# Queuing the prompt's attention visits behind given projection chunks in a gated Conformer and dilated-attention step

## The chip, the cores and the metric

The kernel runs on one core of a Trainium2 chip. TensorE (PE) multiplies matrices, VectorE (DVE), ScalarE (ACT) and GpSimd (POOL) do the elementwise work, SyncE (SP) issues transfers; ScalarE and GpSimd issue transfers too. The metric is the device time of one execution in microseconds, as the median of repeated runs.

## What is computed

One inference step of a decoder layer, for a prompt of 1024 tokens and for 8 sequences of 8 sample tokens (64 columns), with shared weights. Projection, convolution and attention, shortened:

```python
def in_projection(x, w_in, b_in):
    h = jnp.einsum('bsd,de->bse', x, w_in) + b_in
    a_val, a_gate, z_a, q, k, v, z_b, g_a, g_b = jnp.split(h, offs, axis=-1)
    u = a_val * jax.nn.sigmoid(a_gate)
    ...
# branch A: depthwise causal convolution of u, width 31, over 1024 channels
# branch B: 3 groups (window, dilation) = (128,1), (512,4), (2048,16), 8 heads of 64 each
def dilated_prompt(q, k, v, window, dil, slopes):
    s = jnp.einsum('bnirhd,bnjrhd->bnrhij', qb, kk)
    s = jnp.where(valid, s + bias, -jnp.inf)
    lse = jax.nn.logsumexp(s, axis=-1)
    p = jnp.exp(s - lse[..., None])
    o = jnp.einsum('bnrhij,bnjrhd->bnirhd', p, vv)
    ...
def combine_groups(outs, lses):
    w = jax.nn.softmax(jnp.stack(lses, axis=2), axis=2)
    return jnp.sum(w[..., None] * jnp.stack(outs, axis=2), axis=2)
# sample tokens: the same attention over caches of keys and values plus the new tokens' own
# y = LayerNorm(ALPHA * x + W_out(sig(g_a) * W_a(conv * silu(z_a)) + sig(g_b) * W_b(attn * silu(z_b))))
```

## The kernel before

All matmuls of the projections are done in two parts of each operand (`hi` and `lo`, written by ScalarE and VectorE from a loaded weight `raw`), three matmuls for each of 8 depth tiles: 24 matmuls make a *chunk* of 384 or 352 columns of the 1088 (prompt and sample tokens together), and three chunks make one row of output features. A chunk goes to one of three accumulators `mm`, which ScalarE or VectorE empties.

A *unit* is a head pair f (0 to 3) and a group g (0 to 2); its queries and keys are two rows of three chunks (`project_qk`), its values come with those of its group (`project_v`, nine steps a group, stored to DRAM as `vd` and loaded again as `vt`). The attention of a unit goes in *bursts* of query tiles: 4, 3 and 2 bursts for g = 0, 1, 2, so 36 over all units. One *visit* of TensorE does three things in a row: the transposes `PT` of the burst before, the values `O` of the burst before that, and the scores `S` of a new one. Between visits VectorE takes bias and minimum from the scores (`P`, `st`), ScalarE takes the exponentials, and both copy the transposed tiles. When the three groups of an f are done, `combine` weighs them: the scores' minima and sums of groups 1 and 2 are stored by GpSimd (`scr`), loaded again in another layout (`stn`), and VectorE makes `mn`, `e`, `el`, `den` and `w` from them, with one exponential of ScalarE between `e` and `el`; `w` is transposed, stored (`wd`), spread (`wb`) and multiplied into the values.

A *convolution channel block* c (0 to 7) is a gate row (sigmoid on ScalarE into `ub`) and a value row (multiplied into `ub` on VectorE), then 31 taps on VectorE, each a wide one of 1024 elements and a narrow one of 64, into one accumulator slot `cv`. Two slots of `ub` are used in turn: even c has one, odd c the other. Blocks 0 to 4 are recorded after units 2, 4, 6, 8 and 11, blocks 5 to 7 in the sample phase that follows the prompt's attention, where rows of scores over the cached keys (`kv`) stand between projection chunks.

The order on each engine is made by a scheduler that simulates the program with priorities; visits have a high priority, taps a low one. The steps that this text speaks of are, by line: 189 projection matmuls, 349 scores, 378 and 386 transposes and their copies, 402 values, 359 and 366 minima and exponentials, 117 and 118 the splits `hi` and `lo`, 433 the store of the group-2 scores, 449 the load `stn`, 459 the second `mn`, 463 its exponential, 514 the gate's sigmoid, 535 and 538 taps, 552 the sample tokens' own scores, 666 the sample phase's scores.

Of the kernel before, what the change touches and what calls it, by code (L numbers as in the profile page):

```python
# [36 lines left out]
B_CONV = (2, 4, 6, 8, 11)  # L37
# [4 lines left out]
def trunk_kernel(ctx, tc, I, O):  # L42
# [211 lines left out]

    def project_v(g):
# [22 lines left out]
        for t in range(9):  # L278
            ps = mm_ps()
            st = slot(rotate("vst", (12, 13)), [P, 512], n="vst")  # L280
            if t < 8:
# [4 lines left out]
                for i, (a, b) in enumerate(ops):  # L286
                    pe.matmul(ps, a, b, start=(i == 0), stop=(i == len(ops) - 1))  # L287
                dve.tensor_tensor(out=st, in0=ps, in1=vb, op=ALU.add)  # L288
                pool.dma_start(out=vd[g, c], in_=st)
                if t * P >= n0:  # L290
                    pool.dma_start(out=O[f"vt{g}"][t * P - n0:(t + 1) * P - n0], in_=st)
            else:
                ops = [(XP[:, k].rearrange("p a n -> p (a n)"), w[k]) for k in range(KT) for w in (wh, wl)]
                for i, (a, b) in enumerate(ops):
                    pe.matmul(ps, a, b, start=(i == 0), stop=(i == len(ops) - 1))  # L295
# [5 lines left out]
                pool.dma_start(out=O[f"vt{g}"][NP_ - n0:], in_=st[:NS])  # L301

# [132 lines left out]
    def prompt_attention(f, g, q, k, vt, scr):  # L435
# [4 lines left out]
        un = {"g": g, "q": q, "k": k, "vt": vt, "scr": scr, "bias": bias, "st": st, "og": og, "tiles": qtiles(g)}  # L440
        for b in BURSTS[g]:
            visit({"unit": un, "tiles": b})
        return og, st if g == 0 else scr
# [116 lines left out]
    def project_qk(u):  # L560
# [5 lines left out]
        if first:  # L566
            for c0, cn in CHUNKS:
                for (w, ev) in zip(first, evs):
                    ev(0, c0, cn, proj_chunk([(*w, xhi, xlo)], c0, cn))
        else:  # L570
            in_proj(F_Q + i3, evs[0])
            in_proj(F_K + i3, evs[1])
# [9 lines left out]
        qk[u] = new  # L582

    w01 = [(w0, w1)]
    project_qk(0)
    project_qk(1)
    project_v(0)
    credit[1] = 1.7
    for u, (f, g) in enumerate(units):
        if g == 0:  # L590
            res = []
        q, k = qk.pop(u)
        sample_new_scores(f, g, q, k)
        scr = None if g == 0 else dram.tile([NP_, 4], F32, name=nm("scr"))
        res.append(prompt_attention(f, g, q, k, load_v(f, g), scr))
        if g == 0 and todo:
            combine(*todo.pop())
        if u + 2 < len(units):
            project_qk(u + 2)
        if u < 2:  # L600
            project_v(u + 1)
            if u == 1:
# [523 lines left out]
```

## Time and profile before

| | |
|---|---|
| median of 3 runs | 1420.6 us (1413.33 to 1421.51) |
| the profiled execution | 1418.53 us, span 1416.8 us |
| TensorE busy | 1397.8 us (99%) |
| VectorE busy | 844.1 us (60%) |
| ScalarE busy | 444.6 us (31%) |
| GpSimd busy | 159.1 us (11%) |
| mean granted clock of TensorE | 0.997 of full speed |

Busy time is the union of an engine's instructions, and the span goes from the first to the last of them; 1.7 us of the execution lie around the span. Idle time of an engine that others don't wait for costs nothing.

### The profile page before, as it was taken

The page shows a single profiled execution, that of the slowest core. Times are in us where ns is not written, and L with a number is a line of the kernel's source. Part 1 is how long each engine was busy: PE and PEld are TensorE (multiplying, and loading weights), DVE is VectorE, ACT ScalarE, POOL GpSimd, SP SyncE. Part 2 cuts the span into 40 slices and gives each one's busy share as a digit, 9 for nine tenths or more (in the row PEclk, how much of TensorE's full clock was granted, in tenths as well). Part 3 has the DMA queues.
Part 4 walks back from the last instruction along what each step waited for, and adds up shares of the span by engine and source line. Part 5 has one row for each costly group of instructions (what it writes and reads, how often), then busy time and mean ns, then how long its engine had stood idle before and what let it go on. Part 6 is the DMA issues. An engine that isn't in the chain of part 4 may idle for free.

```text
span 1416.8 us, 21922 instructions
## 1 busy us (share of the span) xinstructions
PE 1397.8 (99%) x8682; PEld 1265.6 (89%) x8682; DVE 844.1 (60%) x1632; ACT 444.6 (31%) x984; POOL 159.1 (11%) x302
## 2 busy tenths in 40 slices
PE   9999999999999999999999999999999999999997
PEld 8988888899998899999877878788899999999886
DVE  4223131329958879599989794681267526335686
ACT  5204041234433534346531213122246422103220
POOL 2010111110111110112161302000000000000000
PEclk9999999999999999999999999999999999999999
DMA  6629285266755574665489677686653436434322
GB/s 232 213 102 336 116 305 200 87 223 200 221 179 185 176 224 135 225 202 169 122 257 342 243 274 257 206 303 223 202 187 137 161 111 225 146 93 149 127 90 74
DMA packets 85110, 271.27 MB, mean 191 GB/s; under 512 B 20912, under 2 KB 40688, under 8 KB 83600
## 3 DMA queue, kind: packets, MB, share of 16 engines
q1 hardware_dynamic: 70704, 147.16, 31.8%
q10 hardware_dynamic: 2816, 87.30, 17.5%
q0 software_dynamic: 11488, 35.42, 7.6%
q8 instruction: 68, 1.11, 0.3%
q14 instruction: 34, 0.28, 0.1%
HBM read 236.39 MB, written 120.74 MB: 252 GB/s over the span
## 4 chain that ended last, share of the span: by engine, by line
PE 82%; DVE 9%; DMA 4%; issue 3%; ACT 1%; POOL 0%; SPq 0%; DVEq 0%; ACTq 0%; POOLq 0%
PE mm L189 56%; PE mm L287 9%; PE mm L967 7%; DVE cv L538 4%; PE O L666 2%; PE S L666 1%; PE S L349 1%; PE O L402 1%; PE PT L378 1%; DMA wb<-wd 1%; DVE P L359 1%; ACT P L366 1%; DMA stn<-scr 1%; DVE lo L118 1%; PE mm L295 1%
## 5 line engine op out<-in xcount | busy, mean ns | idle before, releaser
L189 PE MATMUL mm<-x,hi 128*128 128x352 f32 (+1 forms) x3648 | 909.7, 330 | 0.9 <-ACT x L117 0.4
L189 PEld LDWEIGHTS mm<-x,hi 128*128 128x128 f32 x3648 | 641.5, 188 | 43.1 <-issue 23.7
L189 PE MATMUL mm<-x,lo 128*128 128x352 f32 (+1 forms) x1824 | 598.2, 328 | 0.0
L189 PEld LDWEIGHTS mm<-x,lo 128*128 128x128 f32 x1824 | 342.2, 188 | 6.1 <-issue 4.7
L538 DVE SCALAR_TENSOR_TENSOR cv<-ub,conv_w,cv 128x1024 f32<-128x1024 f32 x240 | 306.6, 1278 | 2.0
L117 ACT ACTIVATE hi<-raw 128x1024 fp32r<-128x1024 f32 (+2 forms) x88 | 86.1, 980 | 279.4 <-PE mm L189 239.3
L118 DVE TENSOR_TENSOR lo<-raw,hi 128x1024 fp32r<-128x1024 f32 (+2 forms) x88 | 98.9, 1124 | 112.0 <-ACT hi L117 110.5
L287 PE MATMUL mm<-vhi,x 128*128 128x512 f32 x384 | 119.1, 390 | 0.0
L366 ACT ACTIVATE P<-P,st 128x128 f32<-128x128 f32 (+1 forms) x192 | 84.2, 440 | 73.0 <-DVE st L359 61.7
L287 PEld LDWEIGHTS mm<-vhi,x 128*128 128x128 f32 x384 | 72.1, 188 | 15.1 <-issue 0.2
L288 DVE TENSOR_TENSOR vst<-mm,vb 128x512 f32<-128x512 f32 x24 | 16.6, 692 | 102.9 <-PE mm L287 102.9
L287 PE MATMUL mm<-vlo,x 128*128 128x512 f32 x192 | 74.9, 390 | 0.0
L540 DVE SCALAR_TENSOR_TENSOR cv<-keep,conv_w,cv 128x64 f32<-128x64 f32 x240 | 67.8, 282 | 3.2
L787 ACT ACTIVATE gst<-mm,b_in 128x352 f32<-128x352 f32 (+1 forms) x48 | 26.7, 559 | 114.8 <-PE mm L189 83.3
L359 DVE CUSTOM_DVE_ANT_0 P<-S,bias 128x128 f32<-128x128 f32 (+1 forms) x192 | 55.0, 346 | 10.4 <-PE S L349 10.4
L967 PE MATMUL mm<-wol,mh 128*128 128x512 f32 (+1 forms) x152 | 57.4, 378 | 0.0
L967 PE MATMUL mm<-woh,mh 128*128 128x512 f32 (+1 forms) x152 | 57.4, 378 | 0.0
L967 PE MATMUL mm<-woh,ml 128*128 128x512 f32 (+1 forms) x136 | 51.2, 377 | 0.0
L684 POOL COPY qf<-keep 64x16 f32<-64x16 f32 x96 | 45.9, 490 | 38.7 <-PE S L666 35.4
L287 PEld LDWEIGHTS mm<-vlo,x 128*128 128x128 f32 x192 | 36.0, 188 | 7.5 <-issue 0.2
L378 PE MATMUL PT<-ident,P 128*128 128x128 f32 x280 | 36.9, 274 | 5.5 <-ACT P L366 5.4
L386 DVE COPY PT<-PT 128x512 f32<-128x512 f32 x36 | 24.6, 684 | 28.4 <-PE PT L378 26.1
(185 smaller groups left out, 1309.7 us busy)
## 6 DMA issues: line engine op xcount, KB each, us to landing
out_nb_dram<-in_cache_dram ACTq DMA_DIRECT2D x64, 1020.0 KB
raw<-in_w_in_dram SPq DMA_DIRECT2D x66, 512.0 KB
kv<-in_g3k_dram SPq DMA_DIRECT2D x32, 512.0 KB
kv<-in_g3v_dram SPq DMA_DIRECT2D x32, 512.0 KB
out_nb_dram<-in_cache_dram ACTq DMA_DIRECT2D x16, 1008.0 KB
kv<-in_g2k_dram SPq DMA_DIRECT2D x16, 512.0 KB
kv<-in_g2v_dram SPq DMA_DIRECT2D x16, 512.0 KB
raw<-in_w_v_dram SPq DMA_DIRECT2D x12, 512.0 KB
```

What stands on the lines that cost most here:

```text
L117: h = act.activation(out=dst_hi, in_=src, func=AF.Copy)
L118: dve.tensor_tensor(out=dst_lo, in0=src, in1=dst_hi.bitcast(F32), op=ALU.subtract)
L189: done[0] = pe.matmul(ps[:, :cn], a, b, start=(i == 0), stop=(i == len(ops) - 1))
L287: pe.matmul(ps, a, b, start=(i == 0), stop=(i == len(ops) - 1))
L359: dve.tensor_tensor_reduce(out=pr[:, h, c], in0=ps[:, h, c], in1=un["bias"][:, h, b0:b0 + nk], scale=-1.0, scalar=3e38, op0=ALU.add, op1=A ...
L366: x["exp"] = act.activation(out=pr[:, h, c], in_=pr[:, h, c], func=AF.Exp, scale=-1.0, bias=st[:, t, h, 0:1], accum_out=st[:, t, h, 1:2])
L378: m = pe.transpose(pp[:, i * P:(i + 1) * P], x["pr"][:, h, c:c + P], ident)
L538: dve.scalar_tensor_tensor(out=acc[:, :NP_], in0=ub[:, j:j + NP_], scalar=w, in1=acc[:, :NP_], op0=ALU.mult, op1=ALU.add)
L540: dve.scalar_tensor_tensor(out=accs, in0=us[:, :, j:j + 8], scalar=w, in1=accs, op0=ALU.mult, op1=ALU.add)
L666: m = pe.matmul(ps[rr], w(rr), t(r), start=start, stop=stop, tile_position=(0, rr.start), **kw)
L684: pool.tensor_copy(out=qfull(g)[hs, f].rearrange("p (r j h) -> p r j h", r=4, j=4)[:, :, :, 2 * f + h2], in_=qs[hs, g * 4 + f, 16 * pr:16 ...
L967: pe.matmul(ps[:, :cn], a, b, start=(j == 0), stop=(j == len(ops) - 1))
```

## The change

The visits are no longer placed by the scheduler's priorities. A generator (`beside`) hands out the projections and convolutions in steps, most of them one chunk: values of group g (9 steps) and queries and keys of unit 2+g (6 steps) for g = 0 to 2, then queries and keys of units 5 to 11 with the convolution blocks 0 to 4 among them (`PAIRS`), 6 steps each. Before each burst so many steps are taken that their sum is the number in `VISITS` (from the tenth burst on, 2.75 more for each), and the visit is queued behind the last matmul of the last step. The sample tokens' own scores stand in the first visit of their unit, in an accumulator of the projections and with one store pattern. A unit's values are loaded at its second burst. The combine of f is recorded after the second burst of the next f's first unit. After the last burst two more steps stand before each of the two visits that finish it.

```diff
-B_CONV = (2, 4, 6, 8, 11)
+PAIRS = ((5,), (6, 7), (8, 9), (10, 11), ())
+VISITS = (3, 6, 12, 16, 20, 24, 29, 34, 39)
 W_CONV = ((5,), (6,), (7,), ())
...
     def project_v(g):
...
-                    pe.matmul(ps, a, b, start=(i == 0), stop=(i == len(ops) - 1))
+                    done[0] = pe.matmul(ps, a, b, start=(i == 0), stop=(i == len(ops) - 1))
                 dve.tensor_tensor(out=st, in0=ps, in1=vb, op=ALU.add)
                 pool.dma_start(out=vd[g, c], in_=st)
...
+                yield
...
-    def prompt_attention(f, g, q, k, vt, scr):
+    def prompt_unit(f, g, q, k, scr):
...
-        for b in BURSTS[g]:
-            visit({"unit": un, "tiles": b})
-        return og, st if g == 0 else scr
+        return un, (og, st if g == 0 else scr)
...
     def sample_new_scores(f, g, q, k):
-        t = half("sb", [NS, 2, NS], 2)
-        ps = s_ps()
+        t = half("sb", [P, NS], 2)
+        ps = mm_ps()[:, :NS]
         for h in range(2):
             hs = slice(64 * h, 64 * h + 64)
-            pe.matmul(ps[:NS, h, :NS], q[hs, NP_:], k[hs, NP_:], start=True, stop=True)
-        act.activation(out=t, in_=ps[:NS, :, :NS], func=AF.Copy)
-        pool.dma_start(out=snew[g, 2 * f:2 * f + 2].rearrange("h q k -> q h k"), in_=t)
+            pe.matmul(ps[hs], q[hs, NP_:], k[hs, NP_:], start=True, stop=True)
+        act.activation(out=t, in_=ps, func=AF.Copy)
+        pool.dma_start(out=snew[g, 2 * f:2 * f + 2].rearrange("h q k -> (h q) k"), in_=t)
...
-    project_qk(0)
-    project_qk(1)
-    project_v(0)
-    credit[1] = 1.7
+    def beside():
+
+        for g in range(3):
+            yield from project_v(g)
+            if g == 0:
+                credit[1] = 1.7
+            yield from project_qk(2 + g)
...
+        for c in range(5):
+            for x in PAIRS[c]:
+                yield from project_qk(x)
+            yield from conv_channels(c)
+
+    for u in range(2):
+        for _ in project_qk(u):
+            pass
+    fill = beside()
+    steps = 0
+    n = 0
     for u, (f, g) in enumerate(units):
         if g == 0:
             res = []
-        q, k = qk.pop(u)
-        sample_new_scores(f, g, q, k)
-        scr = None if g == 0 else dram.tile([NP_, 4], F32, name=nm("scr"))
-        res.append(prompt_attention(f, g, q, k, load_v(f, g), scr))
-        if g == 0 and todo:
-            combine(*todo.pop())
-        if u + 2 < len(units):
-            project_qk(u + 2)
...
-        if u in B_CONV:
-            c = B_CONV.index(u)
-            for _ in conv_channels(c):
-                pass
+        for bi, burst in enumerate(BURSTS[g]):
+            n += 1
+
+            while steps < (VISITS[n - 1] if n <= len(VISITS) else VISITS[-1] + 2.75 * (n - len(VISITS))) or (u not in qk):
+                next(fill, None)
+                steps += 1
+            if bi == 0:
+                q, k = qk[u]
+                scr = None if g == 0 else dram.tile([NP_, 4], F32, name=nm("scr"))
+                un, r = prompt_unit(f, g, q, k, scr)
+                res.append(r)
+            elif bi == 1:
+                while ("v", g) not in ready:
+                    next(fill, None)
+                    steps += 1
+                un["vt"] = load_v(f, g)
+            with tc.issue_after(done[0].ins):
+                visit({"unit": un, "tiles": burst})
+                if bi == 0:
+                    sample_new_scores(f, g, q, k)
+            if todo and g == 0 and bi == 1:
+                combine(*todo.pop())
         if g == 2:
             attn[f] = slot(14 + f, [P, NT], n="attn")
             todo.append((f, res))
-    visit()
-    visit()
+    for _ in range(2):
+        for _ in range(2):
+            next(fill, None)
+        with tc.issue_after(done[0].ins):
+            visit()
+    for _ in fill:
+        pass
```

ScalarE at the end of the prompt's attention, with and ahead of the sigmoids of convolution block 5's gate (`mm_712`, `mm_715` and `mm_718` are its three chunks). `P` are exponentials, `PT` and `og` copies, `hi` weight splits, `e_738` and `PT_743` belong to the last combine, `sb` is the copy of the sample tokens' own scores. Before:

```order
L117 ACTIVATE hi_710_6218<-raw_709_6216 128x1024
L384 ACTIVATE PT_651_5725<-PT_653_5732 128x512
L366 ACTIVATE P_656_5753,st_638_5639<-P_656_5753,st_638_5639 128x256 x4
L514 ACT_TABLE_LOAD
L514 ACTIVATE ub_705_6207<-mm_712_6222,b_in_34_198 128x384
L553 ACTIVATE sb_657_5762<-S_658_5763 64x128
L384 ACTIVATE PT_664_5776<-PT_666_5783 128x512
L514 ACTIVATE ub_705_6207<-mm_715_6256,b_in_34_198 128x352
L366 ACT_TABLE_LOAD
```

After:

```order
L120 ACTIVATE hi_710_6218<-raw_709_6216 128x1024
L469 ACTIVATE e_738_6563<-e_738_6563 128x48
L428 ACTIVATE og_660_5766<-O_694_6139 128x8x64
L120 ACTIVATE hi_752_6607<-raw_751_6605 128x1024
L480 ACTIVATE PT_743_6584<-PT_742_6582 48x128
L520 ACT_TABLE_LOAD
L520 ACTIVATE ub_705_6207<-mm_712_6222,b_in_34_198 128x384
L520 ACTIVATE ub_705_6207<-mm_715_6256,b_in_34_198 128x352
L520 ACTIVATE ub_705_6207<-mm_718_6290,b_in_34_198 128x288
```

The sigmoids stood between the last unit's exponentials, and the last combine's exponential came well behind them; now they stand behind the last combine's exponential and the copy of its transposed weights.

VectorE at the same place, around the last combine's `mn_737`. `cv_688` before is block 4's accumulator (it reads `ub_675`, block 4); `cv_656` after is block 3's (it reads `ub_637`). `ub_669` after and `ub_705` before are emptied value chunks of blocks 4 and 5. Before:

```order
L519 SCALAR_TENSOR_TENSOR ub_705_6207<-mm_726_6395,b_in_34_198,ub_705_6207 128x288
L519 SCALAR_TENSOR_TENSOR keep_236_2032<-mm_726_6395,b_in_34_198,keep_236_2032 128x8x8
L538 SCALAR_TENSOR_TENSOR cv_688_6051<-ub_675_5873,conv_w_38_206,cv_688_6051 128x1024
L118 TENSOR_TENSOR lo_766_6712<-raw_764_6709,hi_765_6711 128x1024
L540 SCALAR_TENSOR_TENSOR cv_688_6051<-keep_236_2032,conv_w_38_206,cv_688_6051 128x64
L459 TENSOR_TENSOR mn_737_6562<-mn_737_6562,stn_736_6558 128x16
L538 SCALAR_TENSOR_TENSOR cv_688_6051<-ub_675_5873,conv_w_38_206,cv_688_6051 128x1024
L540 SCALAR_TENSOR_TENSOR cv_688_6051<-keep_236_2032,conv_w_38_206,cv_688_6051 128x64
L461 TENSOR_TENSOR e_738_6563<-mn_737_6562,stn_736_6558 128x16 x3
L538 SCALAR_TENSOR_TENSOR cv_688_6051<-ub_675_5873,conv_w_38_206,cv_688_6051 128x1024
```

After:

```order
L430 COPY og_660_5766<-O_691_6036 128x8x64
L465 TENSOR_TENSOR mn_737_6562<-mn_737_6562,stn_736_6558 128x16
L544 SCALAR_TENSOR_TENSOR cv_656_5698<-ub_637_5482,conv_w_38_206,cv_656_5698 128x1024
L467 TENSOR_TENSOR e_738_6563<-mn_737_6562,stn_736_6558 128x16 x3
L544 SCALAR_TENSOR_TENSOR cv_656_5698<-ub_637_5482,conv_w_38_206,cv_656_5698 128x1024
L525 SCALAR_TENSOR_TENSOR ub_669_5821<-mm_692_6046,b_in_34_198,ub_669_5821 128x288
L525 SCALAR_TENSOR_TENSOR keep_299_2452<-mm_692_6046,b_in_34_198,keep_299_2452 128x8x8
L121 TENSOR_TENSOR lo_711_6219<-raw_709_6216,hi_710_6218 128x1024
L471 TENSOR_TENSOR el_739_6564<-e_738_6563,stn_736_6558 128x16 x3
L544 SCALAR_TENSOR_TENSOR cv_656_5698<-ub_637_5482,conv_w_38_206,cv_656_5698 128x1024
```

The last combine stood among the taps of block 4, behind the last value chunk of block 5; now it stands among the taps of block 3, and the last value chunk of block 4 comes behind it.

ScalarE around the exponential of the first combine (`e_315` before, `e_289` after). `mm_262` is the third chunk of a unit's queries. Before:

```order
L213 ACTIVATE qkv_256_2145<-mm_267_2266,b_in_34_198 128x4x88
L117 ACTIVATE hi_274_2335<-raw_273_2333 128x1024
L154 DMA out_nb2_dram<-in_cache2_dram 16x16320 x2
L213 ACTIVATE qkv_256_2145<-mm_268_2292,b_in_34_198 128x4x72
L213 ACTIVATE qkv_256_2145<-mm_268_2292,b_in_34_198 128x64
L463 ACTIVATE e_315_2727<-e_315_2727 128x48
L514 ACT_TABLE_LOAD
L514 ACTIVATE ub_269_2322<-mm_276_2341,b_in_34_198 128x384
```

After:

```order
L374 ACTIVATE P_253_2126,st_228_1895<-P_253_2126,st_228_1895 128x128 x8
L216 ACTIVATE qkv_255_2144<-mm_260_2154,bq8_216 128x4x96
L216 ACTIVATE qkv_255_2144<-mm_261_2180,bq8_216 128x4x88
L469 ACTIVATE e_289_2413<-e_289_2413 128x48
L120 ACTIVATE hi_303_2457<-raw_302_2455 128x1024
L157 DMA out_nb2_dram<-in_cache2_dram 16x16320 x2
L392 ACTIVATE PT_266_2237<-PT_268_2244 128x512
L216 ACTIVATE qkv_255_2144<-mm_262_2206,bq8_216 128x4x72
L216 ACTIVATE qkv_255_2144<-mm_262_2206,bq8_216 128x64
L559 ACTIVATE sb_272_2274<-mm_273_2275 128x64
```

The exponential stood behind both rows of that unit (`qkv_255`, `qkv_256`) and ahead of a gate; now it stands between the second and the third chunk of the first row, and the copy of the third chunk (`mm_262`) comes behind it.

## Rows read from the trace of the kernel before

**Rows 1.** The page of the profile: its span, part 1 (busy time of each engine, its share of the span, instructions) and the first line of part 4 (the chain that ended last, shares of the span by engine).

```profile
span 1416.8 us, 21922 instructions
...
PE 1397.8 (99%) x8682; PEld 1265.6 (89%) x8682; DVE 844.1 (60%) x1632; ACT 444.6 (31%) x984; POOL 159.1 (11%) x302
...
PE 82%; DVE 9%; DMA 4%; issue 3%; ACT 1%; POOL 0%; SPq 0%; DVEq 0%; ACTq 0%; POOLq 0%
```

**Rows 2.** The waits of TensorE over the whole span: who waited, for what; us in total, times, longest us.

```profile
PE PT L378 <- ACT P L366: 5.4, 3, 3.0
PE S L666 <- DMA kv<-in_g3k_dram: 2.0, 2, 1.0
```

**Rows 3.** TensorE in order of time from 458 to 466 us. Columns: start us, length us, engine, line, operation, output<-inputs, tiles, count, and in brackets the idle time before it and what ended it.

```profile
458.13 0.32 PE L189 MATMUL mm<-x,hi 128*128 128x352 f32 x1
461.43 0.88 PE L378 MATMUL PT<-ident,P 128*128 128x128 f32 x6 [2.97 <-ACT P L366]
462.23 1.83 PE L402 MATMUL O<-PT,vt 128*64 128x128 f32 x16
464.00 2.02 PE L349 MATMUL S<-qkv,qkv 64*128 64x256 f32 x8
```

**Rows 4.** TensorE in order of time, same columns: one visit in mid-kernel, and further on one row of the sample phase's scores.

```profile
656.15 1.03 PE L378 MATMUL PT<-ident,P 128*128 128x128 f32 x8
657.11 1.09 PE L402 MATMUL O<-PT,vt 128*64 128x128 f32 x16
658.13 1.13 PE L349 MATMUL S<-qkv,qkv 64*128 64x256 f32 x8
659.20 0.43 PE L189 MATMUL mm<-x,lo 128*128 128x352 f32 x1
...
700.97 1.06 PE L666 MATMUL S<-kv,qf 128*32 128x512 f32 x8 [0.98 <-DMA kv<-in_g3k_dram]
```

**Rows 5.** Busy time by engine in two stretches (all engines). Columns: stretch, its length, busy us and instructions of PE, PEld, DVE, ACT and POOL, then the granted clock as a share of full speed, DMA share, GB/s.

```profile
462.40:465.80 3.40, 3.40 (x24) 2.45 (x22) 3.37 (x7) 1.45 (x2) 0.00 (x0) 0.50 0.07 22
997.70:1021.80 24.10, 24.10 (x146) 23.71 (x144) 5.76 (x5) 3.78 (x6) 0.53 (x1) 1.00 0.59 196
```

**Rows 6.** The instructions of line 552 (the sample tokens' own scores), and the idle time of their engine before them: us, times.

```profile
L552 PE MATMUL S<-qkv,qkv x48: 218/242/268, 102.6 to 676.8; 64*64 64x64 f32 x48
...
  issue: 2.6, 10
```

**Rows 7.** GpSimd in order of time: the stores of the group-2 scores (`scr`), one per combine, and one load behind them (`stn`). Columns as in rows 3.

```profile
287.68 1.36 POOL L433 DMA_DIRECT2D scr<-st  x2 [16.95 <-ACT P L366]
...
437.29 1.35 POOL L433 DMA_DIRECT2D scr<-st  x2 [6.01 <-ACT P L366]
...
568.47 1.35 POOL L433 DMA_DIRECT2D scr<-st  x2 [11.80 <-ACT P L366]
...
701.14 1.34 POOL L433 DMA_DIRECT2D scr<-st  x2 [18.79 <-ACT P L366]
...
708.93 0.92 POOL L449 DMA_DIRECT2D stn<-scr  x1 [4.45 <-issue]
```

**Rows 8.** VectorE in order of time: the four `mn` steps that wait for the loaded scores.

```profile
305.99 0.17 DVE L459 TENSOR_TENSOR mn<-mn,stn 128x16 f32<-128x16 f32 x1 [12.14 <-DMA stn<-scr]
...
451.21 0.17 DVE L459 TENSOR_TENSOR mn<-mn,stn 128x16 f32<-128x16 f32 x1 [6.64 <-DMA stn<-scr]
...
580.54 0.18 DVE L459 TENSOR_TENSOR mn<-mn,stn 128x16 f32<-128x16 f32 x1 [0.55 <-DMA stn<-scr]
...
717.00 0.17 DVE L459 TENSOR_TENSOR mn<-mn,stn 128x16 f32<-128x16 f32 x1 [3.86 <-DMA stn<-scr]
```

**Rows 9.** VectorE in order of time behind the second of them, same columns.

```profile
451.30 1.28 DVE L538 SCALAR_TENSOR_TENSOR cv<-ub,conv_w,cv 128x1024 f32<-128x1024 f32 x1
452.50 0.34 DVE L461 TENSOR_TENSOR e<-mn,stn 128x16 f32<-128x16 f32 x3
452.75 1.28 DVE L538 SCALAR_TENSOR_TENSOR cv<-ub,conv_w,cv 128x1024 f32<-128x1024 f32 x1
453.95 1.22 DVE L118 TENSOR_TENSOR lo<-raw,hi 128x1024 fp32r<-128x1024 f32 x1
...
459.05 0.17 DVE L467 TENSOR_TENSOR den<-den,el 128x16 f32<-128x16 f32 x1
459.14 0.28 DVE L359 CUSTOM_DVE_ANT_0 P<-S,bias 128x128 f32<-128x128 f32 x1
```

**Rows 10.** How long the transfers take from issue to landing (min, median, max, us): first those of line 433 (`scr`), then those that write `stn`.

```profile
DMA to landing us min/median/max: 5.8/6.8/8.4
...
DMA to landing us min/median/max: 2.7/3.5/8.6
```

**Rows 11.** The last scores of the last unit on TensorE, then the table load and the first of eight exponentials of them on ScalarE (start us, length us, and so on).

```profile
692.08 1.16 PE L349 MATMUL S<-qkv,qkv 64*128 64x128 f32 x16
...
696.36 1.28 ACT L366 ACT_TABLE_LOAD   x1 [1.93 <-DVE st L359]
697.65 0.40 ACT L366 ACTIVATE P<-P,st 128x128 f32<-128x128 f32 x1
```

**Rows 12.** The first tap of convolution block 4 on VectorE, then the first sigmoid of convolution block 5 on ScalarE.

```profile
670.82 0.81 DVE L535 TENSOR_SCALAR cv<-ub,conv_w,conv_b 128x1024 f32<-128x1024 f32 x1 [0.98 <-DMA cvd<-cv]
...
677.94 0.58 ACT L514 ACTIVATE ub<-mm,b_in 128x384 f32<-128x384 f32 x1
```

More of the change, by code (lines that the diff above doesn't have):

```diff
@@ L253, in trunk_kernel @@
     XP = None
+    ready = set()
     def project_v(g):
@@ L294, in project_v @@
                 for i, (a, b) in enumerate(ops):
-                    pe.matmul(ps, a, b, start=(i == 0), stop=(i == len(ops) - 1))
+                    done[0] = pe.matmul(ps, a, b, start=(i == 0), stop=(i == len(ops) - 1))
                 act.activation(out=st[:NS], in_=ps[NS:], func=AF.Copy)
@@ L301, in project_v @@
                 pool.dma_start(out=O[f"vt{g}"][NP_ - n0:], in_=st[:NS])
+                ready.add(("v", g))
+                yield
     def load_v(f, g):
@@ L439, in prompt_attention @@
         og = slot(rotate("O", (8, 9, 10, 11)), [P, NP_], n="og")
-        un = {"g": g, "q": q, "k": k, "vt": vt, "scr": scr, "bias": bias, "st": st, "og": og, "tiles": qtiles(g)}
-        for b in BURSTS[g]:
-            visit({"unit": un, "tiles": b})
-        return og, st if g == 0 else scr
+        un = {"g": g, "q": q, "k": k, "scr": scr, "bias": bias, "st": st, "og": og, "tiles": qtiles(g)}
+        return un, (og, st if g == 0 else scr)
     def combine(f, res):
@@ L569, in project_qk @@
                     ev(0, c0, cn, proj_chunk([(*w, xhi, xlo)], c0, cn))
+                    yield
         else:
-            in_proj(F_Q + i3, evs[0])
-            in_proj(F_K + i3, evs[1])
+            for x, ev in zip((F_Q, F_K), evs):
+                w = load_w(I["w_in"][x + i3], D)
+                for ci, (c0, cn) in enumerate(CHUNKS):
+                    ev(ci, c0, cn, proj_chunk([(*w, xhi, xlo)], c0, cn))
+                    if x == F_Q or ci < 2:
+                        yield
         pool.tensor_copy(out=qs[:, i3, :], in_=new[0][:, NP_:])
@@ L582, in project_qk @@
         qk[u] = new
+        yield
     w01 = [(w0, w1)]
-    project_qk(0)
-    project_qk(1)
-    project_v(0)
-    credit[1] = 1.7
+    def beside():
[4 more added lines that the diff above has]
+            yield from project_qk(2 + g)
+        keep[1] = slot(19, [P, NT], n="keep")
+        usv.extend(keep[i][:, c:c + 304].rearrange("p (b t) -> p b t", b=8) for i, c in ((0, 12 * NS), (1, 0), (1, 304)))
+        for c in range(5):
[8 more added lines that the diff above has]
+    n = 0
     for u, (f, g) in enumerate(units):
@@ L591, in trunk_kernel @@
             res = []
-        q, k = qk.pop(u)
-        sample_new_scores(f, g, q, k)
-        scr = None if g == 0 else dram.tile([NP_, 4], F32, name=nm("scr"))
-        res.append(prompt_attention(f, g, q, k, load_v(f, g), scr))
-        if g == 0 and todo:
-            combine(*todo.pop())
-        if u + 2 < len(units):
-            project_qk(u + 2)
-        if u < 2:
-            project_v(u + 1)
-            if u == 1:
-                keep[1] = slot(19, [P, NT], n="keep")
-                usv += [keep[i][:, c:c + 304].rearrange("p (b t) -> p b t", b=8)
-                        for i, c in ((0, 12 * NS), (1, 0), (1, 304))]
-        if u in B_CONV:
-            c = B_CONV.index(u)
-            for _ in conv_channels(c):
-                pass
+        for bi, burst in enumerate(BURSTS[g]):
[19 more added lines that the diff above has]
+                combine(*todo.pop())
         if g == 2:
```

## The prediction

> **What bounds the kernel now.** I read the page first: TensorE is busy 99% of the span and TensorE work is 82% of the chain that ended last [rows 1], so time is lost or won only where TensorE stands still or runs slowly. Second, the waits of TensorE [rows 2]: over the whole span it waited 5.4 us for exponentials (`P`), 2.0 us for the sample phase's keys (`kv`) and little else. Third, the largest of these waits in order of time [rows 3]: transposes that could have started near 458.4 start at 461.43, and the values and scores behind them take 1.83 and 2.02 us, where the same steps elsewhere take 1.09 and 1.13 [rows 4]. The granted clock says why: 0.50, the lower of the two levels (1.2 GHz), from 462.4 to 465.8, after some 3 us without work [rows 5]. Fourth, what TensorE was waiting for: VectorE stood 6.64 us at `mn L459`, the second step of a combine, until the groups' scores were back from DRAM, and the next visit's scores were queued behind it [rows 8, 9].
>
> So the kernel is a dense stream of projection chunks with visits strewn in; there is little to win, and the question is where the new order puts long waits of VectorE and ScalarE in front of something that TensorE needs.
>
> **What the change removes.** (1) Visits are now 2 to 4 chunks apart. A chunk is 24 matmuls; 146 matmuls of all widths take 24.10 us [rows 5], so 4.0 us for a chunk and 8 to 12 us between visits, in which scores, exponentials and the copy of the transposed tiles fit. The three waits on `P` (5.4 us) and the stretch at half clock should go. The latter cost 1.83+2.02 against 1.09+1.13, that is 1.6 us. (2) The sample tokens' own scores no longer stand alone between projection matmuls: TensorE lost 2.6 us in ten issue gaps ahead of their groups [rows 6]. In a visit these gaps have no reason to exist; I take 2.5. (3) The two waits on `kv`, 2.0 us, belong to visits that stood in the sample phase; I take them as gone here and price what stands there now separately. Sum: 5.4+1.6+2.5+2.0 = 11.5 us. With nothing lost elsewhere that gives 1418.5-11.5 = 1407.0.
>
> **What it moves, and where that waits.** The combine of each f used to be recorded after the whole first unit of the next f; now it comes after that unit's second burst, so its VectorE and ScalarE steps stand closer to the scores that they need. The delay from the issue of the group-2 scores' store on GpSimd to `mn` is in all four combines long: 287.68 to 305.99, 437.29 to 451.21, 568.47 to 580.54, 701.14 to 717.00 [rows 7, 8], which is 18.3, 13.9, 12.1 and 15.9 us, mean 15.0. It is a store, a load behind it on the same queue, and the time that each takes to land [rows 10].
>
> *The handoff to the sample phase (f=3).* Let τ be when TensorE reaches the transposes of the last unit's first burst. From the new order, with 4.0 to 4.1 us for a chunk and 3.05 for a visit [rows 4, 5]: last scores done at τ+18.4 (two visits, three chunks). In the trace 7.9 us went from the end of these scores to the store, 693.24 to 701.14, with a table load and eight exponentials and 1.9 us of waiting for VectorE [rows 7, 11]; with part of that wait I take 6.7: store at τ+25.1, `mn` at τ+40.1 with the mean delay. Behind `mn` VectorE still has 15 wide taps of convolution block 3: six among the steps up to the weights `w`, nine after. By [rows 9] a tap is 1.2 us, a `lo` 1.2 and the small steps 0.1 to 0.3, so the weights are done 10.3 us and the last tap 22.4 us after `mn`: τ+62.5. In the new program the first gate of block 5 (`mm_712`) goes to the ub slot that block 3's taps read, so its sigmoid on ScalarE waits for the last tap; the matmul accumulator that it empties is the one that block 5's first value chunk (`mm_721`) needs (three buffers). With a table load of 1.28 and 0.58 for the sigmoid [rows 11, 12] that chunk starts at τ+64.4. TensorE gets there after nine chunks (36.5), two visits (6.1), a burst's transposes and two bursts' values (3.0) and three rows of sample scores at 1.0 [rows 4], at τ+48.7. So it stands still for 15.7 us; 12.8 with the shortest delay seen, 19.0 with the longest. In the trace before, this did not happen: block 4's first tap, which means the end of block 3's in the one accumulator slot, is at 670.82, and block 5's first sigmoid at 677.94 [rows 12]. I add 1.6 us for a half-clock stretch after the idle, as in [rows 5]. Handoff: 17.3 us (14.4 to 20.6).
>
> On this one length the Trainium skill speaks against my sum: SBUF — State Buffer, section "The DMA setup-cost knee", says that a DMA pays a roughly fixed 2 us however small. An estimate from that page makes two of them with their issues some 6 us, `mn` at τ+31.1, the stall 6.7 us and, with nothing at f=0 and f=2, the whole 1415. The trace disagrees (12.1 to 18.3, landings with medians of 6.8 and 3.5 [rows 10]), and the sum goes by the trace.
>
> *The combine of f=0.* t0 is the end of its last scores. The store goes out at t0+6, `mn` at t0+21 (18.1 to 24.3). On ScalarE its exponential now stands ahead of the emptying of a projection's third chunk (`mm_262`), with a weight split and a copy between; so the accumulator is free at about `mn`+2.9 = t0+23.9. TensorE wants it for `mm_278` after three chunks, a visit and a chunk, t0+19.5: 4.4 us (1.5 to 7.7). Before, the same exponential came when nothing of TensorE was queued behind it that near.
>
> *The combines of f=1 and f=2.* For f=2 `mn` now stands on VectorE ahead of the next burst's scores; their first transpose is due at t0+23.4 and ready 2.65 us after `mn` (0.35 for `mn` and `e`, 2.3 from the first score instruction at 459.14 to the transposes at 461.43 [rows 3, 9]): t0+23.7 at the mean, so 0.3 us, at most 3.6; I take 1. For f=1 visit and combine are far enough apart; nothing.
>
> *At nothing:* the wider store of the sample scores (one pattern of 128x64) and its accumulator buffer, hidden by ScalarE being busy for only 31% [rows 1]; the convolutions themselves, since VectorE is busy for 60%, and a visit interval's share of taps, scores and copies fits the interval within 2 us by the durations in [rows 9]; the values' reloads, 20 us ahead of their use. If that cover fails, it is TensorE time 1:1, which the range carries.
>
> **Sum.** 1418.5-11.5+17.3+4.4+1.0 = 1429.7 with the mean delay. With each f's own delay (18.3 at f=0, 12.1 at f=2, 15.9 at f=3) it is 7.7+0+18.2-11.5 = +14.4, or 1432.9. I take 1431 for the profiled execution's kind of time; the median of the runs before is 1420.6, 2 us above the profiled execution and within the spread of 1413.3 to 1421.5, so I don't shift it. The forecast's own range is 1423 (all delays at 12.1) to 1440 (all at 18.3, and 1 to 2 us for a key tile that is now queued behind loads waiting for the combine).
>
> **The rivals.** *Short delay.* The store and the load now follow each other on GpSimd without copies of the sample queries between. If landings come at their minima, 5.8+0.9+2.7 [rows 7, 10] is about 9.5 us: handoff 10 without much of a clock drop, f=0 nothing, total 1418.5-11.5+10 = 1417. Against it: none of four combines came in under 12.1. The Trainium skill's page above would have it so. *Nothing stalls.* Block 3's taps could run so far ahead of the order's worst case that the slot is free in time; then the gains stand alone, 1407. Against it: the taps stand in VectorE's queue behind `mn`, and no speed of VectorE shortens that. *Longer delay (the other side).* At the handoff the queue of SyncE now issues 22 small loads of the sample scores and four key tiles in the stretch in which the store and the load travel. All three stalls grow 1:1 with the delay, so the time passes 1434.8, 1% above the median, at a delay of 17 us, and at 20 us it is 1418.5-11.5+22.3+9.4+5.3 = 1444. For it: f=0's 18.3 and a load that took 8.6 to land [rows 10]; against it: the mean.
>
> **Chances.** Forecast 0.52, short delay 0.15, nothing stalls 0.12, longer delay 0.21. 1% is about what a measurement of this kernel can tell from no change: 1406.4 to 1434.8. Faster needs the gains alone and a little more: 0.05. Slower is the longer delay, and a quarter of the forecast's own range: 0.34. Within 1%: 0.61. The range 1410 to 1443 leaves out most of "nothing stalls" and the end of the longer delay, some 2 in 10.
>
> **What the profile after would show.** Right: one idle of TensorE of 12 to 19 us at block 5's first value chunk, after the first three rows of sample scores, put down to ScalarE's `ub` sigmoid or VectorE's `cv`, with VectorE idle some 8 us on `stn` just before; a wait of some 4 us at f=0 on `qkv`; no wait on `P` over 1 us; no issue gaps at the sample scores. Wrong: TensorE's waits together under 5 us, or a stall elsewhere, above all on VectorE falling behind the evenly spread visits, or on the values' reload.

## The result and the profile after

The changed kernel takes 1430.87 us (median of 6 runs, 1427.92 to 1434.89) against 1421.05 for the kernel before beside it: 1.0081 times as long, 95% interval 1.0051 to 1.011. The profiled execution took 1428.49 us; its span is 1426.7 us, 9.9 more than before. The forecast was 1431, given for a run like the profiled one.

The page, the lines that answer to [rows 1]:

```profile
span 1426.7 us, 21939 instructions
...
PE 1396.9 (98%) x8682; PEld 1269.5 (89%) x8682; DVE 845.2 (59%) x1632; ACT 442.8 (31%) x982; POOL 184.6 (13%) x302
```

TensorE is busy as long as before (1396.9 and 1397.8 us); what was added to the span is time in which it stands. How much of the busy time is at half clock comes below. Its waits, to be read against [rows 2]:

```profile
PE mm L192 <- ACT ub L520: 8.5, 1, 8.5
PE PT L386 <- ACT P L374: 5.5, 2, 3.9
PE O L410 <- DVE mn L465: 3.7, 1, 3.7
PE S L704 <- DMA kv<-in_g1k_dram: 1.3, 1, 1.3
```

One wait of 8.5 us on the sigmoid of a gate is new, as forecast, and one of 3.7 us ahead of it. But 5.5 us of waiting on exponentials, which the change was to take away, stand there again. The waits in order of time (columns as in rows 3):

```profile
609.68 1.09 PE L386 MATMUL PT<-ident,P 128*128 128x128 f32 x8 [3.91 <-ACT P L374]
610.70 1.76 PE L410 MATMUL O<-PT,vt 128*64 128x128 f32 x16
612.39 2.08 PE L357 MATMUL S<-qkv,qkv 64*128 64x256 f32 x8
...
679.49 1.98 PE L410 MATMUL O<-PT,vt 128*64 128x128 f32 x16 [3.65 <-DVE mn L465]
...
704.24 1.01 PE L192 MATMUL mm<-x,hi 128*128 128x384 f32 x2 [8.50 <-ACT ub L520]
```

The values and scores behind 609.68 take 1.76 and 2.08 us where [rows 4] has 1.09 and 1.13. The granted clock behind each of the three (columns as in rows 5; the clock is the figure ahead of the last two):

```profile
611.00:614.40 3.40, 3.40 (x25) 2.24 (x21) 3.36 (x4) 1.69 (x5) 0.97 (x3) 0.50 0.81 307
679.40:683.00 3.60, 3.51 (x22) 3.21 (x23) 3.60 (x8) 1.31 (x2) 0.28 (x1) 0.55 0.00 0
704.20:710.00 5.80, 5.76 (x18) 5.77 (x19) 0.32 (x1) 1.03 (x3) 2.71 (x6) 0.50 0.69 175
```

It is 0.50 (1.2 GHz) in the first and the third stretch. Of the second, from 679.24, 3.4 us were at half clock too, and of the third 5.7 us of work. Half of the 12 us of work done in such stretches, some 6 us, is lost to the clock; before it was 1.6.

VectorE and ScalarE ahead of the 8.5 us, from the trace in order of time:

```profile
671.63 0.26 DVE L748 CUSTOM_DVE_ANT_0 sb<-sb,bias 128x96 f32<-128x96 f32 x1 [6.88 <-DMA raw<-in_w_in_dram]
...
679.19 0.17 DVE L465 TENSOR_TENSOR mn<-mn,stn 128x16 f32<-128x16 f32 x1
...
697.00 5.24 DVE L544 SCALAR_TENSOR_TENSOR cv<-ub,conv_w,cv 128x1024 f32<-128x1024 f32 x4
...
702.30 1.28 ACT L520 ACT_TABLE_LOAD   x1 [6.20 <-DVE cv L544]
703.60 0.58 ACT L520 ACTIVATE ub<-mm,b_in 128x384 f32<-128x384 f32 x1
```

This is the chain of the forecast, from the taps to the sigmoid: five taps behind the weights, a `lo`, four taps until 702.2, the table load, the sigmoid, and TensorE starts at 704.24. What made VectorE late is another thing than forecast. It stood 6.88 us at line 748, the bias add on the sample tokens' own scores; at `mn` (679.19) it did not wait at all. The row names `raw`, a load that this step does not use; line 748 waits for the scores and their bias. SyncE tells why these came late (its transfers in order of time, and one of its own waits: for what, us, times, longest):

```profile
645.56 16.97 SPq L715 DMA_DIRECT2D sb<-snew  x20
...
663.07 1.28 SPq L715 DMA_DIRECT2D sb<-snew  x2
...
664.89 1.28 SPq L715 DMA_DIRECT2D sb<-snew  x2
666.27 0.39 SPq L711 DMA_DIRECT2D bias<-in_nbias_dram  x1
...
SPq L711 <- DMA bias<-in_nbias_dram: 3.3, 1, 3.3
```

Twenty small loads keep its queue busy for 17 us and four more for 2.6; the bias is issued at 666.27, behind them, and lands at some 671.2, just before VectorE goes on. Line 711, whose next load waits for that landing, names it. In the run below that spreads stored weights the profile puts VectorE's wait at this step (6.73 us) down to the bias itself.

The waits on exponentials lie after the combine of f=2. VectorE, from its wait for the spread weights to the two late score steps:

```profile
569.31 1.23 DVE L489 TENSOR_TENSOR attn<-og,wb 128x1024 f32<-128x1024 f32 x1 [7.77 <-DMA wb<-wd]
...
576.85 0.42 DVE L367 CUSTOM_DVE_ANT_0 P<-S,bias 128x256 f32<-128x256 f32 x1
...
606.03 0.28 DVE L367 CUSTOM_DVE_ANT_0 P<-S,bias 128x128 f32<-128x128 f32 x1
```

For 7.77 us it waited for the weights' way to DRAM and back. After that taps and multiplies stood ahead of the scores, whose exponentials TensorE wanted. VectorE waits so in all four combines (11.3, 7.6, 7.8 and 7.4 us; in the kernel before 0.7, 4.5, 0 and 1.2), but only behind f=2 did a visit come to wait for exponentials.

At f=0 nothing waits. Its store, load and `mn`:

```profile
275.19 1.45 POOL L441 DMA_DIRECT2D scr<-st  x2 [3.71 <-ACT P L374]
279.40 0.91 POOL L455 DMA_DIRECT2D stn<-scr  x1 [2.76 <-issue]
...
282.30 0.18 DVE L465 TENSOR_TENSOR mn<-mn,stn 128x16 f32<-128x16 f32 x1 [4.22 <-DMA stn<-scr]
```

7.1 us, where the kernel before took 18.3 [rows 7, 8].

### The profile page after: what moved, and what is told of

The parts are those of the page before. It is cut to its first block, busy times and chain, and to the rows that moved or that the text cites. A ratio compares the mean times of both kernels' runs of the same rounds, so it can differ in the third digit from the quotient of the medians.

```text
span 1426.7 us, 21939 instructions
## 1 busy us (share of the span) xinstructions
PE 1396.9 (98%) x8682; PEld 1269.5 (89%) x8682; DVE 845.2 (59%) x1632; ACT 442.8 (31%) x982; POOL 184.6 (13%) x302
## 3 DMA queue, kind: packets, MB, share of 16 engines
q10 hardware_dynamic: 2816, 87.30, 17.3%
## 4 chain that ended last, share of the span: by engine, by line
PE 86%; DVE 5%; DMA 3%; issue 3%; POOL 2%; ACT 1%; SPq 0%; DVEq 0%; ACTq 0%; POOLq 0%
PE mm L192 59%; PE mm L292 9%; PE mm L1005 7%; DVE cv L544 2%; PE S L357 2%; PE O L410 2%; PE PT L386 2%; PE O L704 2%; PE S L704 1%; POOL qf L722 1%; DMA wb<-wd 1%; DMA scr<-st 1%; PE mm L301 1%; ACT P L374 1%; PE S L738 1%
## 5 line engine op out<-in xcount | busy, mean ns | idle before, releaser
L722 POOL COPY qf<-keep 64x16 f32<-64x16 f32 x96 | 71.2, 752 | 43.6 <-PE S L704 40.3
L367 DVE CUSTOM_DVE_ANT_0 P<-S,bias 128x128 f32<-128x128 f32 (+1 forms) x192 | 55.0, 350 | 10.2 <-PE S L357 10.2
L410 PE MATMUL O<-PT,vt 128*64 128x128 f32 x560 | 40.1, 287 | 3.7 <-DVE mn L465 3.7
```

The costliest lines, as they stand in the source:

```text
L367: dve.tensor_tensor_reduce(out=pr[:, h, c], in0=ps[:, h, c], in1=un["bias"][:, h, b0:b0 + nk], scale=-1.0, scalar=3e38, op0=ALU.add, op1=A ...
L410: m = pe.matmul(po[64 * h:64 * h + 64, oc], vt[:, vb[j], 64 * h:64 * h + 64], x["pts"][:, place[t, h, j]], start=(j == 0), stop=(j == nb - 1))
L722: pool.tensor_copy(out=qfull(g)[hs, f].rearrange("p (r j h) -> p r j h", r=4, j=4)[:, :, :, 2 * f + h2], in_=qs[hs, g * 4 + f, 16 * pr:16 ...
```

## The experiments

Each ran beside the kernel before on the same chip; the changed kernel stands at ratio 1.0081, and 0.001 of a ratio is 1.4 us. Differences between experiments are taken from the ratios. By the intervals, a difference from the changed kernel of less than some 5 to 7 us is not clear of the noise; what such a run shows is read from its trace.

**Block 5 later.** What does the wait on the sigmoid cost, with all that hangs on it?

```diff
     def filling():
...
+        for _ in range(2):
+            yield from gate_b(*gates.pop(0))
         for cs in W_CONV:
...
```

> The changed kernel, with two rows of merge gates (six chunks, some 24 us) ahead of convolution block 5 in the sample phase; the order of everything else is kept. Theory A (block 5's gate wants the ub slot that block 3's taps still read): the changed kernel's wait of 8.5 us of TensorE on that gate's sigmoid is gone, and with it the 2.9 us that the stretch at half clock behind it cost (5.7 us of work at half speed); 1430.9 becomes 1419 to 1421, ratio to the kernel before 0.999 to 1.001. Theory B (VectorE is late as a whole there, and whatever comes first in the sample phase waits for it): the gates' chunks wait in its place, over 5 us, and the time stays above 1426.

1417.97 us, ratio 0.9986 (0.9968 to 1.0004): 13 us less, a little more than the 11.4 us of theory A; the wait of 1.3 us on a key tile is gone too. Its waits:

```profile
PE PT L386 <- ACT P L374: 5.8, 2, 3.9
PE O L410 <- DVE mn L465: 3.8, 1, 3.8
```

The wait on the sigmoid is gone and nothing of its size has come in its place: the cost was a place in the queue, not VectorE's work as such. Theory A holds. The wait of the last values and those on exponentials are as they were.

**What made the taps late.** Three runs: the bias add moved, the round trip of the group-2 scores taken out, and both.

```diff
+                    last[0] = pe.matmul(s21[:, 256:], qfull(0)[:, f], kt[2][:, f], start=(f == 0), stop=(f == 3))
...
+            if i == 2:
+                tc.add_manual_dep(m.ins, last[0].ins.name, SYNC, reason="behind the scores of the cache")
```

```diff
         for g in (1, 2):
-            pool.dma_start(out=stn[:, g], in_=res[g][1].rearrange("(t p) x -> p t x", p=P))
+            pool.dma_start(out=stn[:, g], in_=res[1][1].rearrange("(t p) x -> p t x", p=P))
```

> The changed kernel, with one step moved on VectorE: the bias add on the sample tokens' own scores (line 748) comes behind the scores over the cache, so that VectorE no longer stands 6.88 us in front of it with block 3's taps behind. Theory A1 (the round trip of the group-2 scores alone sets when the taps end, as the prediction has it): VectorE stands at mn instead, until about 679 us as before; the wait on the sigmoid stays at 7 to 9 us and only the 3.65 us wait of the values before it goes; 1426 to 1428. Theory A2 (the bias add is what set it, and the round trip is done earlier than mn was reached): mn comes 2 to 4 us earlier, both waits together fall from 12.2 to 2 to 6 us, and 1418 to 1423.

1429.57 us, ratio 1.0056 (1.0025 to 1.0087), some 3.5 us less, within the noise. `mn` on VectorE, and where TensorE goes on behind the sigmoid:

```profile
676.04 0.17 DVE L465 TENSOR_TENSOR mn<-mn,stn 128x16 f32<-128x16 f32 x1 [2.95 <-DMA stn<-scr]
...
701.11 1.01 PE L192 MATMUL mm<-x,hi 128*128 128x384 f32 x2 [9.78 <-ACT ub L520]
```

Now VectorE waits at `mn`, but comes to it 3.2 us earlier than in the changed kernel (676.04 against 679.19). The wait of 3.7 us before the gate is gone, the one on the sigmoid grew from 8.5 to 9.8 and the one on a key tile from 1.3 to 3.1, since TensorE reaches both earlier. Theory A2 has `mn` right and the two waits wrong (9.8 us are left): the round trip was 3 us short of being the one that counts, and stands right behind the bias add.

> The changed kernel, where each combine loads the group-1 minima and sums twice instead of those of group 2, so that no combine waits for a round trip of the group-2 scores; it leaves out the weights of group 2. Theory A1 (round trip): the wait on block 5's sigmoid falls to under 3 us and the whole to 1418 to 1422. Theory A2 (bias add of the own scores): the handoff is as before, waits of 3.6 and 8.5 us within 1 us, and the time 1428 to 1432. The waits of 1.6 and 3.9 us on exponentials near 579 and 609 us stay in both, since they come from the weights' way back.

1427.51 us, ratio 1.0057 (1.0032 to 1.0083), some 3.4 us less, within the noise. Its waits, and where TensorE goes on:

```profile
PE mm L192 <- ACT ub L520: 6.8, 1, 6.8
PE PT L386 <- ACT P L374: 5.7, 2, 3.9
PE O L410 <- DVE og L430: 2.8, 1, 2.8
...
704.58 1.01 PE L192 MATMUL mm<-x,hi 128*128 128x384 f32 x2 [6.82 <-ACT ub L520]
```

The waits at the handoff shrink by 2.6 us only, and TensorE goes on behind the sigmoid no earlier than in the changed kernel (704.58 and 704.24). So the round trip by itself is not what set the taps' end: VectorE still stood 4.5 us at the bias add.

> The changed kernel with both waits of VectorE in front of block 3's last taps taken away at once: the bias add on the sample tokens' own scores comes later, and the combines load the group-1 minima and sums twice (the weights of group 2 are left out). Each alone moved the time by only 1 to 3 us. Theory C (two waits in a row, either of which hides the other): VectorE runs through, the taps end 6 to 7 us earlier than in the changed kernel, near 696 us, and the wait on block 5's sigmoid falls to 3 to 6 us with none before it; 1420 to 1425. Theory D (it is neither, the queue of taps alone is too long): the waits together stay over 10 us, 1427 to 1431.

1421.03 us, ratio 1.0017 (0.9998 to 1.0035), some 9 us less, the only one of the three that is clear of the noise. The same rows:

```profile
PE mm L192 <- ACT ub L520: 7.4, 1, 7.4
PE PT L386 <- ACT P L374: 5.2, 2, 3.9
...
698.33 1.01 PE L192 MATMUL mm<-x,hi 128*128 128x384 f32 x2 [7.44 <-ACT ub L520]
```

With both gone the taps end 6 us earlier (TensorE goes on at 698.33 in place of 704.24), and the wait of the values, that on the key tile and one of the three stretches at half clock are gone too. But 7.4 us of waiting on the sigmoid are left: TensorE also arrives 5 us earlier. So two waits stood in a row in front of the taps: with the bias add out of the way the taps end 3 us earlier, with the round trip out of the way no earlier, with both 6 us. The bias add hid the round trip, and the round trip hid half of what the bias add cost, much as theory C has it. Below them there is the plain length of the taps, which C had too short (3 to 6 us of waiting left) and D had as the whole: VectorE runs without a break and is still late for block 5.

**The sample tokens' own scores.**

```diff
-        ps = mm_ps()[:, :NS]
+        ps = s_ps()
...
             if bi == 0:
                 q, k = qk[u]
+                sample_new_scores(f, g, q, k)
...
                 visit({"unit": un, "tiles": burst})
-                if bi == 0:
-                    sample_new_scores(f, g, q, k)
```

> The changed kernel, with the sample tokens' own scores as in the kernel before: in the scores' accumulator, with the old store pattern, free to be placed outside the visit. Theory: a stand-alone pair of these matmuls costs TensorE a re-entry of some 0.2 to 0.4 us in each of 12 units, so 1430.9 becomes 1433 to 1436, and the issue gaps ahead of them are back (2 to 3 us). Rival: the accumulator that they now share with the visits' scores makes visits wait, over 1 us each on S, and the time is above 1438; or the gaps were hidden anyway and the time stays within 1 us of 1430.9.

1434.02 us, ratio 1.0107 (1.007 to 1.0144), 3.7 us more, within the noise. That is the size expected, but not for the reason: the issue gaps came back by 0.9 us only (1.9 in ten places), while the waits on exponentials rose from 5.5 to 9.9 us in four other places. The order of VectorE's work shifted with the edit; what the own scores cost by themselves is not settled by it.

**The weights of f=2.** First the wait alone is taken away, by spreading weights that are long stored; then the multiplies are moved behind it in two ways.

```diff
...
+        wds.append(wd)
+        if f == 2:
+            wd = wds[1]
```

> The changed kernel, where the combine of f=2 spreads the stored weights of f=1 in place of its own, so that VectorE doesn't wait for the way of the weights to DRAM and back (7.77 us before 569 us); it computes the weights of f=2 and leaves them unused. Theory: VectorE's late scores near 577 and 606 us come from that wait, so both waits on exponentials (1.6 and 3.9 us) and the 3.4 us at half clock behind the second are gone; 1430.9 becomes 1423 to 1425. Rival: the evenly spread visits leave VectorE too little time between 577 and 606 us by themselves; the second wait stays at 3 us or more and the time over 1427.

1424.46 us, ratio 1.0033 (1.0012 to 1.0054), some 7 us less. It leaves the weights of f=2 out of the output. Its waits:

```profile
PE mm L192 <- ACT ub L525: 7.4, 1, 7.4
PE S L709 <- DMA kv<-in_g1k_dram: 4.6, 1, 4.6
...
PE PT L386 <- ACT P L374: 0.8, 1, 0.8
```

The waits on exponentials fall from 5.5 to 0.8 us, and the stretch at half clock near 611 us is gone. So they came from VectorE's wait for the weights' way back, and not from the spacing of the visits. A wait on a key tile of the sample phase grew from 1.3 to 4.6 us in exchange.

```diff
+        def spread(behind=None):
...
+                if behind is not None:
+                    tc.add_manual_dep(m.ins, behind.ins.name, SYNC, reason="when the weights are spread")
...
-                combine(*todo.pop())
+                spread = combine(*todo.pop())
+            if f and g == 1 and bi == 1:
+                spread(done[0])
```

> The changed kernel, where the multiplies that spread the weights are queued behind a chunk of the next unit's second burst, a visit or two after the weights have come back. Theory: VectorE no longer stands before them, the two waits on exponentials near 579 and 609 us go, 1423 to 1425. Rival: the outputs' slots are then held longer and the next unit's values wait for them, or the multiplies make VectorE late there instead: over 1427.

1428.77 us, ratio 1.007 (1.0045 to 1.0096): 1.6 us less, within the noise. The waits near 579 and 609 us are gone, but another of 2.1 us stands near 549, behind this row of VectorE:

```profile
548.60 0.17 DVE L465 TENSOR_TENSOR mn<-mn,stn 128x16 f32<-128x16 f32 x1 [7.62 <-DMA stn<-scr]
```

That is the mechanism that the forecast had for f=2: `mn`, waiting for its scores, ahead of the next visit's scores. The handoff did not get shorter.

```diff
-            if todo and g == 0 and bi == 1:
-                combine(*todo.pop())
+        if todo and g == 0:
+            combine(*todo.pop())
```

> The changed kernel with the combine recorded after its unit's last burst, as in the kernel before, and not after the second. Its first steps (mn to the weights) come at the same place on VectorE, its spreading multiplies later. Theory (the early multiplies of f=2 cost the two waits near 579 and 609 us): the first of them falls below 1 us, the whole to 1424 to 1428. Rival (the place in the program is no part of it): 1430 to 1432 and both waits within 0.5 us.

1435.49 us, ratio 1.0108 (1.0069 to 1.0147), 3.8 us more, within the noise. Neither expectation: the waits near 579 and 609 us go, but one of 4.1 us at 552.8 us, again behind `mn`, and longer waits at the handoff outweigh them.

**Put together.** The gates ahead of block 5 and the bias add moved:

> The changed kernel with two rows of merge gates ahead of block 5 and the bias add on the own scores moved behind the cache's scores. With the gates alone the wait of 3.8 us of the last values on VectorE was left, with 3.4 us at half clock behind it. If the bias add set it, both go: 1.4180 ms becomes 1412 to 1414 us, ratio to the kernel before 0.994 to 0.996. If the values waited for VectorE's queue as such, the wait stays over 2 us and the time at 1416 to 1419.

1413.82 us, ratio 0.9964 (0.9948 to 0.998). The wait of the values is gone, as the theory of the bias add has it, and the version is faster than both kernels. Two more, with the combine recorded later and with the multiplies moved:

> The changed kernel with two rows of gates ahead of block 5, the bias add on the own scores behind the cache's scores, and the combine recorded after its unit's last burst. If what each takes away adds up: 1413.8 less the waits on exponentials that were left (4.6 us) and half of 3.4 us at half clock, 1408 to 1410, ratio to the kernel before 0.992 to 0.993. If the late multiplies only move VectorE's lateness, 1413 to 1415.

1417.63 us, ratio 0.9988 (0.9965 to 1.0011), above both expectations: the waits on exponentials rose to 10.7 us, in five places. Recording the combine later is no help here either.

> As the one before it, but with the combine's multiplies queued behind a chunk of the next unit's second burst in place of recording the combine later. If the waits add up: 1408 to 1410, ratio 0.992 to 0.993; if VectorE is late in another place in exchange (a wait of 2.3 us on exponentials near 549 us stood there with the multiplies moved alone): 1411 to 1414.

1411.51 us, ratio 0.9939 (0.991 to 0.9969), the lowest of all medians, some 3.5 us below the version without the moved multiplies. The two intervals overlap, so the order of these two is not shown. Its waits, and VectorE at the `mn` of f=2:

```profile
PE PT L386 <- ACT P L374: 5.2, 2, 3.9
PE S L712 <- DMA kv<-in_g3k_dram: 2.3, 1, 2.3
```

```profile
551.40 0.17 DVE L465 TENSOR_TENSOR mn<-mn,stn 128x16 f32<-128x16 f32 x1 [8.46 <-DMA stn<-scr]
```

Of the changed kernel's 19 us of waiting 7.5 are left, and 3.9 of them are the same exchange as before: the multiplies no longer make VectorE late, and `mn` with 8.46 us does.

## Why the prediction came out, and where its working did not

The median was hit within 1 us and the profiled execution within 3, and the main mechanism, a wait for block 5's sigmoid behind block 3's taps, is the one forecast. That the hit is so close is luck. The sum had 11.2 us on top of the kernel before, and the span grew by 9.9; of the four terms only the handoff came near its size. The gains were some 4 us larger than forecast and f=0 cost 4.4 us less, and f=2 cost 6 us more.

*The gains, 11.5 us:* of the right sign, too small. The old waits on exponentials and keys (7.4 us) and the 1.6 us at half clock are gone from their places. Of the rest, 2.5 us for the own scores' gaps, the profile shows 1.6; their row in the trace after, against [rows 6]:

```profile
  issue: 1.0, 3
```

The sum of what stands in the profile after is 8.5+5.5+3.7+1.3 us of waits and some 6 of half clock, 25 us; the same for before is 5.4+2.0+1.6 = 9.0. The difference is 16 us and the span grew by 9.9, so some 6 us were won elsewhere, in place of 2.5. The busy time says the same: less what the half clock took (6 and 1.6 us) it is 1391 us after and 1396 before, for the same 8682 matmuls. Counted in the traces, TensorE goes 120 times before and 104 times after from the matmuls of projections and output to others, and 12 of the 16 are the own scores. That the 6 us come from these fewer breaks is likely, but no run isolates it.

*The handoff, 17.3 us:* 3.65 and 8.50 us of waits and 4.5 us of half clock, 16.7, with 1.3 on a key tile, which the forecast had in its upper range. Place, sum and the releaser on TensorE are as written, moving block 5 out of the slot's way took 13 us off, and behind `mn` the working holds: the weights are done 10.3 us later, as forecast, and the last tap 23.0 (22.4). But the waits are 12.2 us, not 15.7, and the half clock cost 4.5, not 1.6, so here too a part of the fit is luck. Inside it the working failed at one step: `mn` was put down to the round trip alone (12.1 to 18.3 us after the store). It came 13.3 us after it, but VectorE had been held until 671.63 by the bias add of the own scores, a step that the text did not name, and reached `mn` when the load had landed already. With the bias add moved, `mn` waited for the load and came 9.4 us after the store, less than the shortest delay in the forecast. The rival "longer delay" named the queue of small loads on SyncE as what would slow the round trip; it was that queue, but by its own load, not by slowing others. And the 1.6 us for the clock is too small for a wait of 8.5 us: the half clock lasted 10.2 us, 5.7 of them with work, and cost 2.9.

*f=0, 4.4 us:* nothing. The order is as described, but the delay was 7.1 us, under the shortest of the four before; the range was taken from four delays without asking what the transfer engines carried during them. No run made this delay long, so that the 4.4 us would have come with it is not shown.

*f=2, 1.0 us:* 5.5 us of waits and 1.6 of half clock. The step looked at was `mn`; the one that cost was the multiply behind the weights' way through DRAM and back, which the text did not price. In four of the later versions the step at `mn` does cost 2 to 4 us.

*Chances:* the short delay came true at f=0 only, "nothing stalls" nowhere. Of what the profile after was to show, the wait at block 5's value chunk was there (8.5 us in place of 12 to 19, with 3.65 more before it); VectorE idle on `stn` ahead of it, a wait at f=0 and "no wait on `P` over 1 us" were not.

By an estimate from the Trainium skill's 2 us for a DMA (SBUF — State Buffer, "The DMA setup-cost knee") the store and the load take some 6 us, and the whole 1415. At f=0 after, 7.1 us come close to it; in the six other combines in which `mn` waited for its load it was 12 to 18. The measured delays decide, and the last section has what they go with.

## What to carry to other kernels

When work is put into a fixed order, ask of each in-order engine which of its waiting steps now stands in front of something that the busiest engine needs: list all of them at that place, not only the one that was long in the trace before, since one can hide the next (the taps ended 0 and 3 us earlier with one of two waits gone, 6 with both). A resource handed on late, here a slot that taps still read, can be mended by putting independent work ahead of its next user: six chunks of gates gave back 13 us, more than any of the edits that made the taps earlier. And a total that fits is no proof of its terms.

## What the runs showed of the hardware

The delay of a small store and a load through DRAM was short where the transfer engines were nearly idle. The four combines before, the first three after, and the last one with the bias add moved, all with `mn` waiting for the load (columns as in rows 5; DMA share and GB/s are the last two):

```profile
287.70:306.00 18.30, 18.30 (x125) 17.94 (x124) 1.73 (x3) 3.67 (x8) 3.81 (x6) 1.00 0.69 231
437.30:451.20 13.90, 13.90 (x99) 13.26 (x98) 6.95 (x7) 3.23 (x7) 4.17 (x6) 1.00 0.69 227
568.50:580.50 12.00, 12.00 (x87) 11.66 (x86) 6.19 (x8) 2.72 (x6) 3.39 (x6) 1.00 0.69 192
701.10:717.00 15.90, 14.87 (x114) 11.30 (x110) 10.63 (x18) 2.73 (x3) 9.81 (x27) 1.00 0.91 242
```

```profile
275.20:282.30 7.10, 7.10 (x48) 7.08 (x47) 2.56 (x9) 0.72 (x2) 2.24 (x3) 1.00 0.12 6
403.50:418.50 15.00, 15.00 (x110) 14.23 (x109) 12.81 (x20) 5.18 (x15) 3.78 (x7) 1.00 0.60 201
530.50:543.00 12.50, 12.50 (x95) 11.74 (x94) 4.05 (x5) 4.45 (x7) 2.82 (x4) 1.00 0.49 148
...
666.60:676.00 9.40, 9.40 (x71) 9.04 (x70) 6.42 (x7) 1.66 (x2) 2.25 (x3) 1.00 0.55 125
```

7.1 us at a share of 0.12 and 6 GB/s; 9.4 to 18.3 us at 0.49 to 0.91. In the other versions that load the group-2 scores f=0 is again at 6.9 to 7.3 us with shares of 0.11 to 0.14, and one combine at a share of 0.20 took 8.4 us. Within the upper group the share does not order the delays, so it tells an idle stretch from a loaded one and no more; no run changed the load on purpose.

What a wait costs in half clock behind it is not told by its length. In the changed kernel the granted clock was 0.50 over 3.4 us with the waits of 3.7 and 3.9 us, which cost some 1.6 us each, and with the wait of 8.5 us until 5.7 us of work were done, which cost 2.9. But with the gates ahead of block 5 the same wait of 3.9 us near 611 us has 5.8 us of work at 0.50 behind it (first row). In the version with gates and bias add moved, a wait of 2.28 us has such a stretch behind it and one of 2.27 us has none (second and third row):

```profile
611.10:616.90 5.80, 5.80 (x33) 4.32 (x33) 4.93 (x5) 3.09 (x6) 1.19 (x3) 0.50 0.83 245
...
581.60:584.90 3.30, 3.30 (x23) 2.14 (x19) 3.30 (x4) 1.43 (x4) 3.24 (x4) 0.50 0.01 3
610.40:616.00 5.60, 5.60 (x46) 4.89 (x47) 5.53 (x8) 3.01 (x7) 1.19 (x3) 1.00 0.74 249
```

So waits of 2.3 to 8.5 us cost here between nothing and 2.9 us on top of their length.
